# A hybrid S5 / FNet / attention step on one core: TensorE's queue in the order of the source, the other queues as the scheduler sets them

## The chip, the core and the metric

The kernel runs on one core of one Trainium2 chip. The metric is the device time of one execution in microseconds (us), as the median of several runs.

## What is computed

The reference is one inference step of a model of two layers, for 128 context tokens and 1024 latent tokens of width 1024, in float32. Cut to what matters here, a layer is:

```python
def mixer_layer(x, cvec, lw, ctx_kv, ssm_h0, rope):
    shift, scale, gate = adaln(cvec, ada_w, ada_b)
    h = rmsnorm(x, norm_g) * (1.0 + scale) + shift
    a_in, a_gate, f_in, f_gate, q, k, v, c_gate = jnp.split(h @ w_in, SPLITS, axis=-1)
    ya, finals = s5_mixer(a_in, a_re, a_im, log_dt, b_re, b_im, c_re, c_im, d_skip, h0_f, h0_b)
    za = jax.nn.gelu(ya) @ glu_w
    ya = za[..., :BRANCH_W] * jax.nn.sigmoid(za[..., BRANCH_W:])
    yf = fourier_mix(f_in) @ fnet_w
    q = rmsnorm(q.reshape(b, s, N_HEADS, HEAD_DIM), q_gain)
    k = rmsnorm(k.reshape(b, s, N_KV, HEAD_DIM), k_gain)
    yc = blocked_attention(apply_rope(q, cos, sin), k_all, v_all)
    branches = jnp.stack([ya * silu(a_gate), yf * silu(f_gate), yc * silu(c_gate)], axis=2)
    proj = jnp.einsum('bsnw,nwd->bsnd', branches, w_branch)
    g = jax.nn.sigmoid(h @ merge_w + merge_b)
    return x + gate * (jnp.sum(g * proj, axis=2) @ w_out), k, v, finals
```

So there are large dense products (`w_in`, `glu_w`, `fnet_w`, `merge_w`, `w_branch`, `w_out`) and three branches of many small steps: a state-space branch, a Fourier branch and attention with 8 heads. `adaln` is a product of one vector with a matrix of 1024 x 3072.

## The kernel before

**Tiles.** The 1152 tokens stand in the free dimension in three tiles of 384, the channels on the 128 partitions. Each float32 operand is kept as a rounded part and a remainder (`hh` and `hl`, `whi` and `wlo`), and a product is three matmuls of 128x384 (`mm3`, L162). A block of dense output is made in units by the generator `dense` (L269): weights are loaded (`wst`), split by ScalarE (`whi`) and GpSimd (`wlo`), and after each 12 matmuls into a `pd` buffer it yields. An evacuation on ScalarE or VectorE (`jo`) and a DMA follow each `pd`.

**PSUM.** There are four names of buffers: `pd` (2, dense), `pt` (2), `pv` (1) and `pa` (1, three banks). The three branches and the setup share `pt`, `pv` and `pa`.

**What is traced.** The branches are generators too, and `drive` (L92) traces two or three of them in turn by the costs that they yield. The stages of a layer (`layer`, L1289) are: dense blocks beside the state-space setup, state inputs and scans; `qkv_gen` (L837) beside dense blocks; `ssm_out_gen` (L738) beside dense blocks; `glu`; `fnet_gen` (L1001) beside three dense blocks; `attn_gen` (L1089) with the merge blocks, 12 matmuls between two steps; the output blocks beside the norm of the next layer (`h_gen`, L470). `run` (L1541) traces the head ahead of that: the constants, the loads of x, one step of `ada_gen` (L306), the transposes of x (`x_gen`, L398), the rest of `ada_gen` with the first normalized tiles.

**What sets the order.** The tracing order is not the order of the queues. The scheduler of the tile framework takes the traced instructions and sets the order of each engine's queue by its own model of when they get ready and when buffers come free. On TensorE that moves dense matmuls between the steps of a branch and branch steps between dense matmuls.

The lines that the change touches are `mm` (L167), which issues every matmul, and `tr` (L170), which issues every transpose; the helpers `act` (L134), `tt` (L144) and `stt` (L147) for ScalarE, VectorE and GpSimd, and `dma` (L124), stay as they are. Steps named further on:

- `qkv_gen`: `tail()` (L912) transposes the rotated heads of one token tile (`qk_kk`, `qk_qt`) into `pa`, copies them out (`qk_qo`) on ScalarE and stores them. The tail of tile t-3 is traced after the projection of tile t. The last ones follow each other in the trace.
- `fnet_gen`: for each of four channel groups, load `fn_X`, even and odd sums `fn_EO` (six operations on VectorE), an alternating sum `fn_s`, folded sums `fn_G` (eight operations), the channel transform into `pt`, its split `fn_AB`, the position transform into `pa`, and the sums of the result (`fn_s`, `fn_X` again) with the split into `A`.
- `ssm_out_gen`: coefficients `ss_CK` on VectorE, `toeplitz` (L763) with small matmuls into `pt`, a way through DRAM (`tpd`) back as `ss_TT`, a copy `ss_TP`, the output products into `pa` and `pv`.
- `attn_gen`: `scores` (L1112) into `pa`, a softmax (`at_mx`, `at_P`), `trans` (L1123) with nine transposes, and for each second step `pvm` (L1135).
- `h_gen`: the sum of squares (`ssq`) by `ones` into `pv`, the scales `rs`, their transposes.

Of the kernel before, what the change touches and what calls it, by code (L numbers as in the profile page):

```python
# [101 lines left out]
class Program:  # L102
# [62 lines left out]
        self.mm(out, w[1], x[0], False, last)  # L165

    def mm(self, out, w, x, first=True, last=True, **kw):  # L167
        return self.nc.tensor.matmul(out, w, x, start=first, stop=last, **kw)  # L168

    def tr(self, out, in_, ident=None):  # L170
        i = self.ident if ident is None else ident
        n = in_.shape[0]
        return self.nc.tensor.transpose(out, in_, i[:n, :n])  # L173


    def setup(self):
# [1418 lines left out]
```

## Time and profile before

| | us |
|---|---|
| median of 3 runs (2752.75 to 2756.11) | 2754.29 |
| the profiled execution | 2752.03 |
| its span, first to last instruction | 2750.3 |
| TensorE matmuls and transposes busy | 2627.0 (96%) |
| TensorE weight loads busy (beside the matmuls) | 2509.0 (91%) |
| VectorE | 1826.6 (66%) |
| ScalarE | 1143.5 (42%) |
| GpSimd | 683.4 (25%) |

The mean granted TensorE clock is 0.985 of full speed. PE stands for TensorE, DVE for VectorE, ACT for ScalarE, POOL for GpSimd, SP for the engine that issues most DMAs. A wait is the idle time of an engine just before an instruction; the name behind the arrow is what ended last before it. A row of the timeline gives start and length in us; neighbours of one kind are drawn together with their count, and the ends of matmuls overlap the next start, so starts tell the pace.

### The profile page before, as it was taken

How to read it: one execution, taken by the hardware profiler on the slowest of the kernel's cores; microseconds unless marked ns; L12 is line 12 of the kernel's file. 1: busy time of each engine (PE TensorE's matmuls, PEld its weight loads, DVE VectorE, ACT ScalarE, POOL GpSimd, SP SyncE). 2: the span in 40 equal slices, each digit the busy share in tenths (PEclk: the TensorE clock that was granted, in tenths of full speed). 3: DMA queues.
4: the chain of work that ended last, by engine and by line, in shares of the span. 5: the costliest groups of instructions: out<-in, count | busy, mean ns of one | idle time of the engine just before them, and what ended most of it. 6: DMA issues, size and time to landing. Idle time of an engine off the chain costs nothing. (4 is left out here: it accounts for less than half of the span.)

```text
span 2750.3 us, 44553 instructions
## 1 busy us (share of the span) xinstructions
PE 2627.0 (96%) x16092; PEld 2509.0 (91%) x16092; DVE 1826.6 (66%) x3933; ACT 1143.5 (42%) x2676; POOL 683.4 (25%) x521
## 2 busy tenths in 40 slices
PE   7998999899999999999999899999999999999998
PEld 3898999799999999999989899989989998999998
DVE  6549955856558889866572797577654788891343
ACT  5461145331355565423345322543223655553244
POOL 3241122322321020132343212233222202102223
PEclk9999999999999999999999999999999999999999
DMA  6632223566263345544543222345645334433244
GB/s 223 178 99 84 95 87 110 150 191 207 86 202 114 110 138 153 173 126 114 165 146 93 95 89 84 107 125 160 211 154 174 109 121 150 143 121 98 80 121 149
DMA packets 459997, 366.85 MB, mean 133 GB/s; under 512 B 72953, under 2 KB 432001, under 8 KB 459777
## 3 DMA queue, kind: packets, MB, share of 16 engines
q1 hardware_dynamic: 458480, 359.75, 42.9%
q0 software_dynamic: 1296, 4.26, 0.5%
q8 instruction: 127, 2.08, 0.3%
q14 instruction: 94, 0.76, 0.1%
HBM read 243.52 MB, written 120.39 MB: 132 GB/s over the span
## 5 line engine op out<-in xcount | busy, mean ns | idle before, releaser
L168 PE MATMUL pd<-hh,whi 128*128 128x384 f32 x2496 | 857.1, 344 | 24.0 <-ACT jo L142 20.1
L168 PE MATMUL pd<-hh,wlo 128*128 128x384 f32 x2496 | 844.6, 339 | 3.2 <-POOL wlo L145 3.2
L168 PE MATMUL pd<-hl,whi 128*128 128x384 f32 x2496 | 843.1, 338 | 1.3 <-DVE hl L149 1.3
L145 POOL TENSOR_TENSOR wlo<-wst,whi 128x512 fp32r<-128x512 f32 x312 | 437.9, 1405 | 1525.8 <-ACT whi L142 1404.8
L168 PEld LDWEIGHTS pd<-hh,whi 128*128 128x128 f32 x2496 | 472.5, 189 | 35.0 <-ACT jo L142 22.8
L168 PEld LDWEIGHTS pd<-hh,wlo 128*128 128x128 f32 x2496 | 472.5, 189 | 7.8 <-POOL wlo L145 5.7
L168 PEld LDWEIGHTS pd<-hl,whi 128*128 128x128 f32 x2496 | 473.1, 190 | 3.8 <-DVE hl L149 2.3
L168 PE MATMUL pd<-A,whi 128*128 128x384 f32 x1728 | 458.2, 342 | 8.2 <-ACT jo L142 4.9
L168 PEld LDWEIGHTS pd<-A,whi 128*128 128x128 f32 x1728 | 311.2, 189 | 11.7 <-ACT jo L142 5.6
L142 ACT ACTIVATE whi<-wst 128x512 fp32r<-128x512 f32 x312 | 196.0, 630 | 278.5 <-PE pd L168 190.6
L168 PE MATMUL pd<-A,wlo 128*128 128x384 f32 x864 | 293.9, 340 | 0.0
L1078 DVE TENSOR_REDUCE at_mx<-pa 128x1 f32<-128x1152 f32 x128 | 173.3, 1354 | 16.1 <-PE pa L168 15.7
L168 PE MATMUL pa<-at_K,at_Q 128*128 128x384 f32 x768 | 167.2, 347 | 8.6 <-ACT at_P L142 5.8
L142 ACT ACTIVATE at_PT<-pt 128x384 fp32r<-128x384 f32 (+1 forms) x260 | 114.9, 490 | 144.0 <-PE pt L173 143.6
L142 ACT ACTIVATE at_P<-pa,at_mx 128x1152 f32<-128x1152 f32 x128 | 158.1, 1235 | 20.7 <-DVE at_mx L1078 19.4
L168 PEld LDWEIGHTS pd<-A,wlo 128*128 128x128 f32 x864 | 163.2, 189 | 0.1
L168 PEld LDWEIGHTS pa<-at_K,at_Q 128*128 128x128 f32 x768 | 128.3, 188 | 29.0 <-ACT at_P L142 25.5
L168 PE MATMUL pt<-qkW,hh 128*128 128x384 f32 x576 | 150.7, 343 | 0.0
L168 PE MATMUL pv<-at_PT,at_V 128*128 128x256 f32 x1152 | 148.8, 283 | 0.0
L168 PEld LDWEIGHTS pv<-at_PT,at_V 128*128 128x128 f32 x1152 | 144.7, 191 | 0.8
L142 ACT ACTIVATE jo<-pd 128x384 f32<-128x384 f32 x120 | 58.0, 485 | 198.1 <-PE pd L168 96.5
L145 DVE TENSOR_TENSOR at_PT<-pt,at_PT 128x384 fp32r<-128x384 f32 (+1 forms) x260 | 133.1, 550 | 10.0 <-ACT at_PT L142 7.8
(294 smaller groups left out, 3772.3 us busy)
## 6 DMA issues: line engine op xcount, KB each, us to landing
aw<-in_ada_w_dram SPq DMA_DIRECT2D x48, 512.0 KB, 4.8
wst<-in_merge_w_dram SPq DMA_DIRECT2D x96, 256.0 KB, 3.0
wst<-in_w_in_dram SPq DMA_DIRECT2D x80, 256.0 KB, 2.9
td<-jo SPq DMA_DIRECT2D x96, 192.0 KB, 2.3
jt<-td SPq DMA_DIRECT2D x96, 192.0 KB, 2.8
wst<-in_w_out_dram SPq DMA_DIRECT2D x64, 256.0 KB, 2.9
sgd<-jo SPq DMA_DIRECT2D x72, 192.0 KB, 2.0
jt<-sgd SPq DMA_DIRECT2D x64, 192.0 KB, 2.7
```

The costliest lines, as they stand in the source:

```text
L142: return self.nc.scalar.activation(out, in_, func, **kw)
L145: return (e or self.nc.vector).tensor_tensor(out=out, in0=a, in1=b, op=op)
L168: return self.nc.tensor.matmul(out, w, x, start=first, stop=last, **kw)
L1078: nc.vector.tensor_reduce(out=mx[:, 0:1], in_=src, axis=AX.XY if m3 else AX.X, op=OP.max, negate=True)
```

## The change

Every matmul and every transpose that the program traces is handed to `keep_in_program_order`: TensorE's queue then has these instructions in the order in which the source traces them. Nothing else is pinned; VectorE, ScalarE, GpSimd and the DMA queue get their orders from the scheduler as before. No instruction is added and none is taken away.

```diff
     def mm(self, out, w, x, first=True, last=True, **kw):
-        return self.nc.tensor.matmul(out, w, x, start=first, stop=last, **kw)
+        return self.tc.keep_in_program_order(self.nc.tensor.matmul(out, w, x, start=first, stop=last, **kw))
 
     def tr(self, out, in_, ident=None):
         i = self.ident if ident is None else ident
         n = in_.shape[0]
-        return self.nc.tensor.transpose(out, in_, i[:n, :n])
+        return self.tc.keep_in_program_order(self.nc.tensor.transpose(out, in_, i[:n, :n]))
```

What this does to TensorE's queue is shown at three places, first before and then with the change. In these rows `pt`, `pv`, `pa` and `pd` are the PSUM buffers that are written.

The head, from the queue's second row on: `ident,hl_77` to `hl_79` are the transposes of x (24 for each tile of 384 tokens), `fvst` that of the small vectors, `aw,silc` and `awr,sc` the matmuls of `ada_gen` with its weights. Before:

```order
L173 MATMUL pt<-ident,hl_77 128x128 x8
L173 MATMUL pv<-ident,fvst 128x128
L173 MATMUL pt<-ident,hl_77 128x128 x16
L173 MATMUL pt<-ident,hl_78 128x128 x24
L173 MATMUL pt<-ident,hl_79 128x128 x24
L168 MATMUL pa<-aw,silc 4x512
L168 MATMUL pa<-awr,sc_108 4x512 x2
```

With the change:

```order
L173 MATMUL pv<-ident,fvst 128x128
L168 MATMUL pa<-aw,silc 4x512
L173 MATMUL pt<-ident,hl_77 128x128 x24
L173 MATMUL pt<-ident,hl_78 128x128 x24
L173 MATMUL pt<-ident,hl_79 128x128 x24
L168 MATMUL pa<-awr,sc_108 4x512 x2
L168 MATMUL pa<-aw,silc 4x512
```

The first matmul of `ada_gen` has moved from behind the 72 transposes of x to ahead of them.

The last tails of the first half of `qkv_gen` in layer 0, with the numbers of the buffers: `pa_4580` to `pa_4670` are the tails of the last four tiles, `pv_4694` that of the cached keys, `pd_4726` is a dense block. Before:

```order
L173 MATMUL pa_4580<-identr_81,qk_kk_4441 128x128 x4
L173 MATMUL pa_4580<-identr_81,qk_qt_4438 128x128 x2
L168 MATMUL pd_4726<-hh0_345,whi_4037 128x384
L168 MATMUL pd_4726<-hl0_346,whi_4037 128x384
L168 MATMUL pd_4726<-hh0_345,wlo_4038 128x384
L168 MATMUL pd_4726<-hh0_345,whi_4037 128x384
L168 MATMUL pd_4726<-hl0_346,whi_4037 128x384
L168 MATMUL pd_4726<-hh0_345,wlo_4038 128x384
L168 MATMUL pd_4726<-hh0_345,whi_4037 128x384
```

With the change:

```order
L173 MATMUL pa_4580<-identr_81,qk_kk_4441 128x128 x4
L173 MATMUL pa_4580<-identr_81,qk_qt_4438 128x128 x2
L173 MATMUL pa_4623<-identr_81,qk_kk_4528 128x128 x4
L173 MATMUL pa_4623<-identr_81,qk_qt_4525 128x128 x2
L173 MATMUL pa_4657<-identr_81,qk_kk_4611 128x128 x4
L173 MATMUL pa_4657<-identr_81,qk_qt_4608 128x128 x2
L173 MATMUL pa_4670<-identr_81,qk_kk_4654 128x128 x4
L173 MATMUL pa_4670<-identr_81,qk_qt_4651 128x128 x2
L173 MATMUL pv_4694<-identr_81,qk_kk_4691 128x128 x4
```

The dense block and the projection of the second half's first tile, which stood between the tails, have moved behind the last of them.

The Fourier stage of layer 0, at the end of a group: `dftp,fn_ABp` is the last matmul of the group's position transform, `dftc,fn_G` the first of the next group's channel transform, `pd` a dense block. Before:

```order
L168 MATMUL pa<-fn_t_7175,fn_AB 128x2x128
L168 MATMUL pa<-dftp,fn_ABp 128x128 x2
L168 MATMUL pd<-hh_347,whi 128x384
L168 MATMUL pd<-hl_348,whi 128x384
L168 MATMUL pd<-hh_347,wlo 128x384
L168 MATMUL pd<-hh_347,whi 128x384
```

With the change:

```order
L168 MATMUL pa<-fn_t_7175,fn_AB 128x2x128
L168 MATMUL pa<-dftp,fn_ABp 128x128 x2
L168 MATMUL pt<-dftc,fn_G 128x128 x4
L168 MATMUL pd<-hh_347,whi 128x384
L168 MATMUL pd<-hl_348,whi 128x384
L168 MATMUL pd<-hh_347,wlo 128x384
```

Before, some 40 dense matmuls stand between the two groups; with the change the next group's first four transform matmuls follow at once, and in the two later groups 12 dense matmuls stand between.

## Rows read from the trace of the kernel before

**Rows 1.** The page: span, and busy time of each engine

```profile
span 2750.3 us, 44553 instructions
...
PE 2627.0 (96%) x16092; PEld 2509.0 (91%) x16092; DVE 1826.6 (66%) x3933; ACT 1143.5 (42%) x2676; POOL 683.4 (25%) x521
```

**Rows 2.** Waits of PE, whole kernel: line <- awaited: us in total, times, longest

```profile
PE pd L168 <- ACT jo L142: 25.1, 8, 7.8
...
PE pt L173 <- DVE at_P L1082: 8.4, 13, 1.0
...
PE pt L168 <- DVE fn_G L145: 6.3, 9, 0.9
```

**Rows 3.** Windows: us, PE PEld DVE ACT POOL busy, PEclk, DMA share, GB/s

```profile
49.60:63.30 13.70, 9.83 (x20) 2.40 (x21) 8.18 (x15) 7.24 (x14) 10.46 (x7) 0.50 0.42 116
220.30:230.50 10.20, 5.57 (x17) 5.57 (x18) 9.61 (x34) 1.60 (x4) 1.27 (x1) 0.50 0.20 64
418.30:421.70 3.40, 3.40 (x15) 3.40 (x14) 3.05 (x8) 1.37 (x4) 1.19 (x1) 0.50 0.52 155
414.00:428.50 14.50, 11.99 (x72) 11.21 (x71) 8.13 (x22) 8.10 (x27) 4.52 (x4) 0.88 0.65 188
432.00:442.00 10.00, 10.00 (x60) 10.00 (x59) 3.50 (x8) 5.03 (x27) 1.33 (x1) 1.00 0.18 56
2030.00:2100.00 70.00, 67.08 (x430) 64.58 (x429) 36.95 (x94) 23.60 (x50) 22.96 (x14) 1.00 0.33 106
```

**Rows 4.** Timeline, PE, Fourier stage: start us, length us, instruction [idle before]

```profile
696.68 0.60 PE L168 MATMUL pa<-dftp,fn_ABp 128*128 128x128 f32 x4
...
713.98 0.61 PE L168 MATMUL pa<-dftp,fn_ABp 128*128 128x128 f32 x4
...
727.81 0.60 PE L168 MATMUL pa<-dftp,fn_ABp 128*128 128x128 f32 x4
```

**Rows 5.** Timeline, DVE, the same stage: the fn_G of three groups

```profile
703.55 5.08 DVE L145 TENSOR_TENSOR fn_G<-fn_EO 128x192 f32<-128x192 f32 x8
...
720.87 2.92 DVE L145 TENSOR_TENSOR fn_G<-fn_EO 128x192 f32<-128x192 f32 x8
...
735.80 3.97 DVE L145 TENSOR_TENSOR fn_G<-fn_EO 128x192 f32<-128x192 f32 x8
```

**Rows 6.** Timeline, PE, tails of q/k/v in layer 0

```profile
414.17 0.46 PE L173 MATMUL pa<-identr,qk_kk 128*128 128x128 f32 x4
...
414.64 0.41 PE L168 MATMUL pd<-hh,whi 128*128 128x384 f32 x1
...
428.08 0.34 PE L173 MATMUL pv<-identr,qk_kk 128*128 128x128 f32 x2
```

**Rows 7.** Timeline, PE, head

```profile
8.48 1.94 PE L173 MATMUL pt<-ident,hl 128*128 128x128 f32 x8 [8.48 <-DMA dmask<-in_k_dmask_dram]
...
24.50 1.02 PE L168 MATMUL pa<-aw,silc 128*4 128x512 f32 x2
...
52.80 0.59 PE L168 MATMUL pa<-awr,sc 128*4 128x512 f32 x1 [3.60 <-POOL awr L145]
```

**Rows 8.** Timeline, PE, state-space output of layer 0

```profile
487.65 1.03 PE L168 MATMUL pt<-ss_CK,ss_B 128*32 128x240 f32 x8 [3.36 <-issue]
...
505.91 0.51 PE L168 MATMUL pa<-ssU,ss_TP 128*128 128x145 f32 x2 [0.98 <-ACT ss_TP L142]
...
532.40 0.76 PE L168 MATMUL pa<-ss_Hg,ss_CA 128*128 128x145 f32 x4 [2.32 <-DVE ss_Hg L805]
```

**Rows 9.** Lines, 766 to 1145 us: instruction, shapes, count | busy us, mean ns | idle

```profile
L1078 DVE TENSOR_REDUCE at_mx<-pa 128x1 f32<-128x1152 f32 x64 | 86.6, 1354 | 8.0 <-PE pa L168 7.8
...
L142 ACT ACTIVATE at_P<-pa,at_mx 128x1152 f32<-128x1152 f32 x64 | 79.0, 1235 | 10.4 <-DVE at_mx L1078 9.7
```

**Rows 10.** Timeline, PE, two long waits

```profile
224.93 0.69 PE L168 MATMUL pd<-hh,whi 128*128 128x384 f32 x1 [7.84 <-ACT jo L142]
...
1412.53 1.41 PE L168 MATMUL pv<-ones,ssq 128*128 128x1 f32 x6 [4.20 <-DVE ssq L145]
```

## The prediction

> **What bounds the kernel now.** I read the page's head and block of busy times first. TensorE matmuls are busy 2627.0 us of a span of 2750.3 us [rows 1]: TensorE is the bound nearly everywhere, and all its idle time together is 123 us. A better order could win at most that, and most of it stands in a few places; an order that leaves TensorE standing where it now works costs one for one. Next come the waits of TensorE [rows 2]. They are short: the largest sum is 25.1 us in 8 waits for a copy of ScalarE, then waits of about 0.7 us each in attention and in the Fourier stage. So the chains that run over VectorE, ScalarE and a DMA are hidden now, because the scheduler put dense matmuls (`pd`) between the steps of a chain. The question is what each chain hides behind when the steps of TensorE stand as they are traced. The orders of the changed kernel answer where: on VectorE, ScalarE, GpSimd and the DMA queue the chains stand nearly as before, and on TensorE the order is the same in most dense stretches, but not in the head, at the tails of q/k/v, at the start of the state-space output, in the Fourier stage, in attention and at the end of a layer. Last I read the granted clock [rows 3]: at full clock 60 matmuls and transposes take 10.0 us (0.167 us each, 2.0 us for a dense piece of 12), and after waits there are stretches at 0.50 (1.2 GHz), where they take about twice as long.
>
> **What the change does, place by place.** It adds and removes no arithmetic; the work displaced from one place is done in another. What it costs is the TensorE time that is not covered any more, at full clock.
>
> *Fourier stage, twice.* For three of the four channel groups the chain is: last `pa` matmul, then VectorE's `fn_s`, `fn_X`, `fn_EO`, `fn_s`, then eight `fn_G` subtractions, each feeding two transform matmuls into `pt`. The `pa` rows end at 697.28, 714.59 and 728.41 (start plus length) [rows 4]. The first of the eight `fn_G` is done at 703.55 + 5.08/8 = 704.2, at 720.87 + 0.37 = 721.2 and at 735.80 + 0.50 = 736.3 [rows 5]: chains of 6.9, 6.6 and 7.9 us, together 21.4. Before, dense pieces filled them. In the pinned order 0, 12 and 12 dense matmuls stand there, 4.0 us by the row of rows 3; 17.4 us stay open. Eight `fn_G` take 5.08, 2.92 and 3.97 us against some 2 us of matmuls that wait for them; beyond the first op and the piece of 12 that now stands inside the first group that is another 2.3. Against 19.7 stand the waits that are there already, 6.3 us in both layers [rows 2], 3.2 a layer. **+16.5 a layer**, ends 12 (the chain shorter, since no dense evacuations are on VectorE meanwhile) and 23 (nothing of the 4.0 helps).
>
> *Tails of q/k/v, twice.* Transposes of rotated heads into the one `pa` buffer stand at 414.17 and three places more, and `pv` ends it at 428.08 [rows 6]. Between two of them lie ScalarE's copy `qk_qo` and the stores. In these 14.5 us TensorE was busy 11.99 [rows 3], 2.0 of it the transposes themselves (six within 0.47 us, to the dense row at 414.64 [rows 6], four times, and the `pv`). The other 10.0 us were dense and q-projection matmuls, 3.4 us of that at clock 0.50 [rows 3], so worth 8.3 at full clock. All of it now stands behind the last transpose. **+9 a layer**, ends 6 (the copies come faster when ScalarE has no dense evacuations) and 12.
>
> *Head, once.* The first ada matmul is traced before the transposes of x and now stands ahead of all 72. It needs the first weight tile, which is loaded behind x; it ran without a wait at 24.50, after transposes that began at 8.48 [rows 7], so the tile was there somewhat earlier. If the transposes begin at 22 to 24 in place of 8.48, and take most of the 16.0 us that they took there, they end at 36 or later. Part comes back: ada waited 3.60 at 52.80 [rows 7] and ran 13.7 us at half clock [rows 3], which with weights waiting in place may go. **+8**, ends 2 (half clock gone too) and 16 (the whole 24.50 - 8.48).
>
> *State-space output, twice.* Products of `ss_CK` into `pt` stand between dense pieces from 487.65 to 505.91, with waits of 3.36 and 0.98 in the rows [rows 8]; four second halves of dense pieces (8 us) now stand behind. The later wait of 2.32 at 532.40 [rows 8] takes some back: **+5 a layer**, ends 2 and 8.
>
> *Attention, twice.* Between the scores of one step and the transposes of the step before lie a maximum of 1.354 us and an exponential of 1.235 us [rows 9] and the scaling; two or three dense matmuls fewer cover it on every other step. It waits now 13 times for the scaled probabilities, 8.4 us in all [rows 2], so the cover is nearly exact. **+3 a layer**, ends 0 and 10.
>
> *End of a layer.* The 4.20 us wait for `ssq` at 1412.53 [rows 10] stays; the transposes of the scale rows move up behind it. **+3**, ends 1 and 7.
>
> *Clock.* A wait that is now bare can be followed by a stretch of 3.4 us at 0.50 as at 418.3 [rows 3], which loses 1.7. The tails, the head and the state-space output have theirs already. The Fourier stage has none in layer 1, where the clock was 1.00 for 70 us [rows 3], so I take four new ones: **+7**, ends 0 and 34 (below).
>
> The clock rule of the Trainium skill speaks against the change: its page "TensorE: Matmul & The Clock Gate", section "HAM oscillation — how this bites in real kernels", says that waits between bursts of matmuls throw the array back to half rate burst after burst. The trace agrees only in part: in those 70 us TensorE stood still for 2.92 [rows 3], and the clock stayed at 1.00; by the rule the sum is the fourth rival's, by the row it is mine.
>
> **The sum.** 2 x 16.5 + 2 x 9 + 8 + 2 x 5 + 2 x 3 + 3 + 7 = +85. The profiled execution took 2752.03 us (span 2750.3, 1.7 around it), 2.3 below the median of 2754.29; put on the median it is **2839 us**. All low ends together give +43, all high ends but the clock's +136; 8 in 10 of this case lie in 2808 to 2870.
>
> **The rivals.** *First, faster.* The two longest waits of TensorE, 7.84 us at 224.93 [rows 10] and its like in layer 1, end with ScalarE's copy `jo`, which stands behind other copies in ScalarE's queue. The scheduler of ScalarE sees another TensorE order and might put `jo` first. That gives back 15.7 us, and the two stretches of 10.2 us at half clock there [rows 3] another 10: with no new bare wait 2754 - 26 = 2728 us. It decides only while the new waits stay under 26 us, and in the changed order ScalarE has these copies where they were. *Second, the chains are shorter than they look,* because their lengths in the trace hold dense evacuations on the same engines: all terms at their low ends but the Fourier stage at 10, +39, 2793 us. For: `fn_X` and `fn_G` vary by nearly two (5.08 against 2.92 us [rows 5]). Against: their shortest sum is still over 5 us. *Third, attention opens.* If each of the 64 pairs of steps loses 0.8 us in place of 13 losing 0.65, this is +51 in place of +6: 2884 us. Against: every second step keeps a value product in between, and the dense piece of each step stays between its transposes and the next scores. *Fourth, the clock falls after each bare wait:* some 20 new ones (6 Fourier, 8 tails, 4 state-space, head, end of layer) times 1.7 is +34 in place of +7: 2866 us. *Fifth, the pin does nothing,* 2754 us: against it, TensorE's order differs, and a queue that waited 7.84 us in one place does not go round a waiting matmul.
>
> **How the numbers follow.** Forecast 0.55, second 0.18, fourth 0.12, third 0.08, first 0.04, fifth 0.03. The range 2785 to 2890 takes in the forecast's bounds, the second and the fourth, and part of the third; outside are the first, the fifth, a slice of the second and of the third. A difference under 0.2% (5.5 us) can't be told from none. Faster by more: the first and a trace of the second, 0.05; within: the fifth and a little, 0.04; slower: the rest, 0.91.
>
> **What would show it.** Right: TensorE's busy time about as before and its idle time about 200 us; waits for `fn_G` or `fn_s` of 5 to 8 us, six times, the largest of all; waits for `qk_qo` above 15 us in sum; the first transposes of x behind the first ada matmul; some 35 to 50 us of the loss before the end of layer 0's Fourier stage. Wrong: waits for `fn_G` under 2 us each (the dense pieces still cover), waits for `at_P` above 30 us (third), or the 7.84 us gone (first).

## The result and the profile after

The changed kernel takes 2903.56 us (median of 4 runs, 2900.02 to 2908.60) against 2753.64 us of the kernel before in the same comparison: a ratio of 1.0544, 95% interval 1.0526 to 1.0563, some 150 us slower. The direction was as forecast; the forecast of 2839 us and the upper end of the range, 2890, were too low.

The page of the profiled execution after, with the head and the busy times that answer to [rows 1]:

```profile
span 2906.8 us, 44552 instructions
...
PE 2648.2 (91%) x16092; PEld 2542.3 (87%) x16092; DVE 1808.2 (62%) x3933; ACT 1147.6 (39%) x2676; POOL 673.6 (23%) x521
```

TensorE's busy time has risen by 21 us (2648.2 against 2627.0) and its idle time within the span by 135 us (258.6 against 123.3). VectorE, ScalarE and GpSimd do the same work in a longer span. The mean granted clock fell from 0.985 to 0.965.

TensorE's waits after, by what they ended with (total us, times, longest), which answer to [rows 2]:

```profile
PE pt L168 <- DVE fn_G L145: 42.2, 9, 7.1
PE pd L168 <- ACT jo L142: 25.5, 8, 7.8
PE pa L173 <- ACT qk_qo L142: 24.5, 8, 5.8
PE pa L168 <- DMA aw<-in_ada_w_dram: 12.9, 1, 12.9
PE pv L173 <- DMA ss_ld<-in_ssm_a_re_dram: 12.8, 1, 12.8
...
PE pv L168 <- DVE at_PT L145: 9.2, 17, 0.8
...
PE pa L168 <- ACT ss_TP L142: 7.9, 2, 4.0
PE pa L168 <- DVE ss_Hg L805: 7.8, 6, 2.4
PE pa L173 <- ACT A L142: 7.7, 4, 1.9
PE pt L173 <- ACT A L142: 7.7, 4, 1.9
PE pv L168 <- DVE ssq L145: 6.6, 1, 6.6
...
PE pt L173 <- DVE at_P L1082: 5.4, 7, 1.5
```

The wait for `jo` is the same as before (25.5 against 25.1). That for `fn_G` went from 6.3 to 42.2. Most of the others in this list were shorter or absent before (`qk_qo` 5.8 in sum, `ss_TP` 1.6, `ssq` 4.2, `ss_Hg` 6.4); that for `at_P` fell, from 8.4 to 5.4.

Where the time came in is read from the starts of TensorE's instructions: at the borders of the stages both queues have the same matmul at the same place, so the time between two such starts can be compared. The profiled execution after is the slowest of its four (2908.60 us), so these differences add up to 156.5 us, where the medians are 150 apart. "Idle" is the sum of TensorE's waits in a stretch; "rest" is what remains of the difference, which is matmuls that ran slower.

| stretch of the kernel before, us | what runs there | before | after | more | of it idle | rest | forecast |
|---|---|---|---|---|---|---|---|
| 0 to 140 | head, first dense blocks | 140.1 | 163.0 | 22.9 | 24.1 | -1.2 | 8 |
| 405 to 470 | tails of q/k/v, layer 0 | 65.0 | 74.5 | 9.6 | 8.2 | 1.3 | 9 |
| 480 to 600 | state-space output, layer 0 | 120.1 | 127.8 | 7.8 | 5.7 | 2.1 | 5 |
| 690 to 765 | Fourier stage, layer 0 | 75.1 | 94.9 | 19.7 | 17.8 | 2.0 | 16.5 |
| 765 to 1150 | attention, layer 0 | 384.9 | 391.8 | 6.9 | 6.8 | 0.0 | 3 |
| 1400 to 1540 | end of layer 0 | 139.9 | 146.2 | 6.2 | 6.6 | -0.5 | 3 |
| 1750 to 1780 | tails of q/k/v, layer 1 | 30.0 | 39.4 | 9.4 | 8.9 | 0.6 | 9 |
| 1822 to 1910 | state-space output, layer 1 | 87.7 | 96.5 | 8.9 | 6.5 | 2.3 | 5 |
| 2025 to 2110 | Fourier stage, layer 1 | 84.9 | 108.1 | 23.2 | 16.6 | 6.6 | 16.5 |
| 2110 to 2495 | attention, layer 1 | 385.0 | 394.7 | 9.6 | 8.5 | 1.2 | 3 |
| 2695 to the end | last output blocks, final norm | 55.1 | 75.7 | 20.6 | 14.2 | 6.3 | 0 |

The other stretches together make 12 us, 5 of them from 1150 to 1400 us. The clock, which the forecast counted by itself with 7, is in the column of the rest.

**Fourier stage.** TensorE's timeline at three of the group ends (start, length, instruction, idle before), which answers to [rows 4]:

```profile
739.10 0.60 PE L168 MATMUL pa<-dftp,fn_ABp 128*128 128x128 f32 x4
746.41 0.77 PE L168 MATMUL pt<-dftc,fn_G 128*128 128x128 f32 x2 [6.71 <-DVE fn_G L145]
...
759.07 0.60 PE L168 MATMUL pa<-dftp,fn_ABp 128*128 128x128 f32 x4
...
768.69 3.76 PE L168 MATMUL pt<-dftc,fn_G 128*128 128x128 f32 x16 [6.93 <-DVE fn_G L145]
...
780.11 0.60 PE L168 MATMUL pa<-dftp,fn_ABp 128*128 128x128 f32 x4
...
789.36 3.75 PE L168 MATMUL pt<-dftc,fn_G 128*128 128x128 f32 x16 [6.56 <-DVE fn_G L145]
```

From the end of the last `pa` matmul to the first `fn_G` matmul it takes 6.7, 9.0 and 8.6 us (739.70 to 746.41, 759.67 to 768.69, 780.71 to 789.36), against chains of 6.9, 6.6 and 7.9 that were read from the trace before. TensorE's waits just ahead of these `fn_G` matmuls are 6.71, 6.93 and 6.56; in the second and third gap the 12 dense matmuls fill the rest.

**Head.** TensorE's timeline, and then the DMA queue's, from the first ada matmul to the first transpose of `ss_ld`, with the queue's longest wait from 50 to 95 us as the last line; it answers to [rows 7]:

```profile
23.06 1.87 PE L168 MATMUL pa<-aw,silc 128*4 128x512 f32 x2 [12.86 <-DMA aw<-in_ada_w_dram]
...
38.16 0.66 PE L173 MATMUL pt<-ident,hl 128*128 128x128 f32 x4 [0.35 <-DVE A L415]
...
91.72 0.28 PE L173 MATMUL pv<-ident,ss_ld 32*128 32x32 f32 x1 [12.84 <-DMA ss_ld<-in_ssm_a_re_dram]
```

```profile
63.26 5.83 SPq L127 DMA_DIRECT2D xTd<-A  x6
89.78 0.33 SPq L127 DMA_DIRECT2D ss_ld<-in_ssm_a_re_dram  x1
...
SPq L127 <- DVE hl L149: 20.1, 1, 20.1
```

The first ada matmul ran at 23.06, after a wait of 12.86 for its weights, and the transposes ended near 38.8 in place of 24.5. Then comes a second wait, 12.84 at 91.72, for the load of `ss_ld`. The DMA queue issued that load at 89.78, 20 us after the last of the stores ahead of it. Before the change it was issued at 82.35 and the transposes ran at 85.14, without a wait, with dense matmuls ahead of them. What held the queue in those 20.1 us was VectorE: the wait ends with the last `hl` of the head's normalized tiles, written from 88.07 to 89.22. I read it as a buffer in memory that the head uses until then (the load goes out late in both kernels); the buffer was not tried by itself.

**Last output blocks.** TensorE's timeline of three blocks after and then of two before:

```profile
2860.73 0.55 PE L173 MATMUL pa<-ident,A 128*128 128x128 f32 x3 [1.91 <-ACT A L142]
...
2868.93 0.55 PE L173 MATMUL pa<-ident,A 128*128 128x128 f32 x3 [1.91 <-ACT A L142]
...
2875.57 0.44 PE L173 MATMUL pt<-ident,A 128*128 128x128 f32 x2 [1.91 <-ACT A L142]
```

```profile
2718.12 0.54 PE L173 MATMUL pa<-ident,A 128*128 128x128 f32 x3
...
2722.68 0.54 PE L173 MATMUL pa<-ident,A 128*128 128x128 f32 x3
```

Each transposes the result of the dense block just finished, as it was traced. Ahead of it TensorE waits 1.91 us, for an evacuation on VectorE, then a square and a scaling on ScalarE. A block then takes 6.64 us (2868.93 to 2875.57), and 8.20 where the clock was low (2860.73 to 2868.93); in the kernel before, with the transposes one piece of 12 matmuls later, 4.56. These two blocks of the pinned kernel as windows (as in [rows 3]; the granted clock is the third number from the end):

```profile
2860.73:2868.93 8.20, 6.29 (x28) 5.97 (x28) 1.67 (x3) 2.40 (x4) 2.55 (x2) 0.79 0.31 93
2868.93:2875.57 6.64, 4.73 (x28) 4.41 (x28) 1.67 (x3) 2.40 (x4) 2.55 (x2) 1.00 0.34 102
```

### The profile page after: what moved, and what is told of

The parts are those of the page before. It is cut to its first block, busy times and chain, and to the rows that moved or that the text cites. A ratio compares the mean times of both kernels' runs of the same rounds, so it can differ in the third digit from the quotient of the medians.

```text
span 2906.8 us, 44552 instructions
## 1 busy us (share of the span) xinstructions
PE 2648.2 (91%) x16092; PEld 2542.3 (87%) x16092; DVE 1808.2 (62%) x3933; ACT 1147.6 (39%) x2676; POOL 673.6 (23%) x521
## 5 line engine op out<-in xcount | busy, mean ns | idle before, releaser
L168 PE MATMUL pd<-hh,whi 128*128 128x384 f32 x2496 | 867.2, 347 | 21.8 <-ACT jo L142 20.2
L168 PEld LDWEIGHTS pd<-hh,whi 128*128 128x128 f32 x2496 | 478.9, 192 | 32.4 <-ACT jo L142 23.2
L142 ACT ACTIVATE at_P<-pa,at_mx 128x1152 f32<-128x1152 f32 x128 | 158.4, 1237 | 12.9 <-DVE at_mx L1078 12.7
L168 PEld LDWEIGHTS pv<-at_PT,at_V 128*128 128x128 f32 x1152 | 141.8, 191 | 19.5 <-ACT at_P L142 15.5
```

The source lines that it names most:

```text
L142: return self.nc.scalar.activation(out, in_, func, **kw)
L168: return self.tc.keep_in_program_order(self.nc.tensor.matmul(out, w, x, start=first, stop=last, **kw))
```

## The experiments

Each kernel below is compared with the kernel before in its own runs; "us against the pinned kernel" is the difference of the two ratios (to 1.0544) times 2754. The 95% interval of most ratios is some 5 us wide to either side, so a difference from the pinned kernel under about 7 us can't be told from none.

**1. The head.** In the pinned kernel:

```diff
-            next(ada)
             self.run_all(self.x_gen(xT, ssq))
+            next(ada)
```

> The pinned kernel, with the first ada step traced behind the transposes of x in place of ahead of them; all else pinned. Theory (the pinned order costs what is bare behind an instruction that waits, place by place): the 12.9 us wait for the first weight tile and the late transposes go, the ada matmuls end about 10 us sooner; the later wait of 12.8 us for ss_ld stays. 2903.6 - 10 = 2893 us. Rival (the head is bounded by its weight loads whatever the order): within 3 us of 2903.6, with the same time of the first dense matmul.

Measured 2899.47 us, ratio 1.0513 (1.0480 to 1.0546): about 9 us less, which its wide interval doesn't set clear of noise. The trace does: just behind the head TensorE's instructions start 9.3 us sooner (6.1 of it is left at the end), and the wait for `ss_ld` is 13.36 us. So the head has two costs of about that size, and this takes away one.

**2. The last output blocks.** The transposes of block b (`tails(b)` traces the three) stand where block b+1 is evacuated:

```diff
+                            if b:
+                                tails(b - 1)
+                            if b == 7:
+                                tails(7)
...
-                            for i in range(3):
-                                self.tr(self.tail[i][b // 4][:, 128 * (b % 4):128 * (b % 4) + 128], xo[:, b, 768 + 128 * i:896 + 128 * i])
```

> The pinned kernel, with the transposes of the last output blocks traced one dense block later, so that 24 dense matmuls stand between an evacuation and the transposes that read it. Theory: the waits of 1.9 us before these transposes (seven in the last stage) and the half clock behind them go; TensorE's lag on the kernel before grows by 20 us in this stage, so 2903.6 - 18 = 2886 us. Rival (the lag comes from the clock or from the queues of the other engines): under 5 us.

Measured 2888.34 us, ratio 1.0483 (1.0464 to 1.0502): 17 us less. The blocks stand 4.5 us apart again:

```profile
2853.51 0.49 PE L173 MATMUL pa<-ident,A 128*128 128x128 f32 x3
...
2858.01 0.49 PE L173 MATMUL pa<-ident,A 128*128 128x128 f32 x3
```

**3. The Fourier stage left to the scheduler,** all else pinned:

```diff
+            self.pin = False
             drive((self.dense(3), 48), (self.fnet_gen(l, f_d, zt["f"]), 48))
+            self.pin = True
```

> The pinned kernel, with the instructions of the Fourier stage (three dense blocks and the Fourier branch, both layers) not pinned, so that the scheduler sets them. Theory: the 42 us waits for fn_G fall to the 6 of the kernel before, both layers give back 19 and 23 us: 2903.6 - 40 = 2864 us. Rival (what is won there is lost later, at the head of attention): 2885 or more.

Measured 2865.40 us, ratio 1.0398 (1.0377 to 1.0418): 40 us less. The row of its waits for `fn_G` (`pin` adds lines, so numbers shift) is that of the kernel before:

```profile
PE pt L169 <- DVE fn_G L146: 6.3, 9, 0.9
```

**4. Bare waits filled.** Behind a group's last `pa` matmul, for three groups of each layer:

```diff
+            if g < 3:
+                fill = self.pst("pv")
+                for i in range(24):
+                    self.mm(fill[:, :384], self.dftl[0][:, 0, :128], self.hh[0][:, 0])
```

> The pinned kernel with 24 more matmuls, whose result nobody reads, in each of the three bare waits of the Fourier stage of each layer. They take 4.1 us of a wait of 6.6 to 7 us at full clock. Theory with a share of the clock: the waits stay covered, the stretches at half clock behind them (24 us in layer 0, 20 in layer 1) go, and with them 8 to 20 us: about 2890 us. Rival (the clock has no share, the chain on VectorE alone paces the stage): 2901 to 2906. Third (the waits were no free room): 24 more, 2928.

Measured 2910.10 us, ratio 1.0563 (1.0540 to 1.0587): 5 us more, within the noise, and in none of the three expected ranges; the nearest is the rival's. The windows (us, five engines' busy times, granted clock, DMA) of the same stretch of the pinned kernel, and then of this one:

```profile
745.00:755.00 10.00, 8.10 (x40) 7.79 (x41) 5.40 (x13) 2.22 (x5) 2.53 (x2) 0.64 0.05 20
...
765.00:775.00 10.00, 6.31 (x32) 6.32 (x33) 6.49 (x20) 1.20 (x2) 1.71 (x2) 0.66 0.08 25
```

```profile
745.00:755.00 10.00, 6.83 (x36) 6.62 (x37) 5.90 (x16) 1.96 (x5) 3.50 (x2) 0.83 0.03 10
...
765.00:775.00 10.00, 6.47 (x29) 6.18 (x29) 7.63 (x19) 2.29 (x4) 3.53 (x3) 0.70 0.14 46
```

The clock is higher, 0.83 in place of 0.64, but the stage isn't shorter: the group ends stand 19.5, 22.7 and 20.5 us apart (740.07, 759.53, 782.22, 802.67) against 20.0, 21.0 and 20.6. So 144 matmuls more, about 25 us at 0.173 us each, cost about 5: the waits are room (those for `fn_G` fall from 42.2 to 19.4 us). It suggests that the low clock behind them costs little here, because the stage goes by VectorE's chain. But the filler also moves the dense pieces and their evacuations deeper into that chain, so this doesn't measure the clock's share. How much of the whole loss is due to the clock is not settled: the "rest" of the table, some 21 us in all, is what slower matmuls added to TensorE's busy time.

**5. The tails of q/k/v** between the projections of the second half (`cl`, `ch` and `cp` are the tails, projections and code carried over from the first half):

```diff
+                if half and t < 3:
+                    cl.pop(t + 6)()
+                    if t == 0:
+                        cl[8] = cp(8, *ch.pop(8))
+                    yield 400
```

> The pinned kernel, with the last three tails of q/k/v's first half and that of the cached keys traced between the projections of the second half, so that each has a projection of 24 matmuls between it and the next. Theory (bare waits, place by place): the 24 us waits for qk_qo go, both layers give back 9.5 us, 2903.6 - 17 = 2887 us. Rival (the copies and stores of the tails bound the stage): under 5 us.

Measured 2905.63 us, ratio 1.0545 (1.0529 to 1.0561): nothing. TensorE's waits in the tails of layer 0, pinned kernel and then this one:

```profile
PE pa L173 <- ACT qk_qo L142: 10.7, 3, 5.8
```

```profile
PE pv L173 <- ACT qk_kk L142: 5.4, 1, 5.4
PE pt L168 <- POOL qkW L145: 1.5, 2, 0.9
PE pt L168 <- ACT qkW L142: 1.4, 1, 1.4
```

The waits for `qk_qo` went. In their place stand the cached keys (5.4: their split and transposes are traced together) and the weights of the second half (`qkW`). I read the second as a matter of buffers: `qkW` has one set, its split starts when the first half's last projection ends, and the bare tails had covered it. That was not tried by itself; experiment 9, which changes both, loses under 1 us in these stretches.

**6. The state-space output** left to the scheduler:

```diff
+                    self.pin = False
                     drive((self.dense(6), 12*6), (self.ssm_out_gen(l, a_d, y_d), 33), (self.qtail_gen(), QT))
+                    self.pin = True
```

> The pinned kernel, with the state-space output stage (six dense blocks, the branch and the last q tails, both layers) left to the scheduler. Theory: the 8.6 and 9 us lost there come back, 2903.6 - 15 = 2888 us. Rival (the loss there is a loss by the clock or is taken back at the next stage): 2898 or more.

Measured 2891.35 us (2886.89 to 2899.06), ratio 1.0503 (1.0477 to 1.0529): 11 us less. In its profiled execution, one of its two fastest, some 8 us come back at the stage in layer 0 and 9 at that in layer 1; the spread of its runs is larger than that of most others, and the median shows less.

**7. The Fourier stage pinned alone,** the rest left to the scheduler:

```diff
-        self.pin = True
+        self.pin = False
...
+            self.pin = True
             drive((self.dense(3), 48), (self.fnet_gen(l, f_d, zt["f"]), 48))
+            self.pin = False
```

> The kernel before, with the instructions of the Fourier stage alone pinned. Theory (each place costs for itself): as much more than the kernel before as the pinned kernel loses there, 19 + 23 us: about 2796 us. Rival (the loss needs the pinned neighbours): under 2770.

Measured 2799.01 us, ratio 1.0157 (1.0140 to 1.0174): 43 us more than the kernel before. Its trace lies 2 us behind that of before at 679 us, 21 at 750, 26 at 2033 and 49 at 2098. The place costs for itself what it costs in the pinned kernel.

**8. Attention and merges** left to the scheduler:

```diff
+            self.pin = False
             for k in self.attn_gen(l, qs_d, k_d, v_d, sg_d[2], zc_d):
                 self.run_some(m, k)
             run(m)
+            self.pin = True
```

> The pinned kernel, with attention and the merge blocks beside it left to the scheduler, both layers. Theory: the 7 and 10 us lost there come back, 2903.6 - 16 = 2888 us. Rival (attention drifts by some us with the phase in which it starts, whatever the order): 2897 or more.

Measured 2895.62 us, ratio 1.0511 (1.0493 to 1.0530): 9 us less, just clear of noise, between theory and rival. The first layer gives back 6 to 7 us, the second 2 to 4. In the pinned kernel the value product waits 9 times, 5.0 us, for the last split `at_PT` in layer 0 alone; here once, for 1.4, but the wait for `at_P` rises from 2.7 to 6.7. So which wait makes attention's loss is not shown.

**9. The source traced anew at six places,** still pinned: experiments 1, 2 and 5 (the cached keys two projections later, a higher cost yielded while the second half's weights are split), and three other costs:

```diff
+        if l == 0:
+            yield 830
-            yield 2000 if x == 0 else 1200
+            yield 4500 if x == 0 else 3000 if x == 1 else 700
-            yield 500
+            yield 6000 if g else 500
```

(`ssm_setup_gen`, `ssm_out_gen`, `fnet_gen`; a yielded cost decides how many dense pieces `drive` traces next. Two further such costs, in `fnet_gen` and in the share of `ssm_setup_gen` in `drive`, are changed too and not printed.)

> The pinned kernel with its source traced anew at six places, so that dense matmuls stand in the bare waits: the first ada step behind the transposes of x, the transposes of ss_ld six dense pieces later, the tails of q/k/v between the projections of the second half (and that of the cached keys two projections later), three pieces between two Fourier groups, more pieces ahead of the first products of the state-space output, the transposes of the last output blocks one block later. Theory (a pinned order is as good as the order in which the source is traced): of the 150 us some 110 come back, what stays is attention, 17, and the ends of layers: 2785 to 2805 us. Rival (the pinned order costs by itself, since nothing answers to waits any more): above 2840.

Measured 2807.89 us, ratio 1.0191 (1.0174 to 1.0208): 97 us less, just above the theory's range. TensorE's waits:

```profile
PE pd L168 <- ACT jo L142: 25.6, 8, 7.8
PE pa L168 <- ACT ss_TP L142: 15.1, 4, 4.1
PE pt L168 <- DVE fn_G L145: 11.0, 7, 2.8
...
PE pv L168 <- DVE at_PT L145: 9.5, 18, 0.5
...
PE pa L173 <- ACT qk_qo L142: 5.0, 4, 1.5
```

`fn_G` is down to 11.0, `qk_qo` to 5.0, `ss_ld` and `aw` are out of the list. `ss_TP` rose from 7.9 to 15.1: as I read it, more dense pieces ahead of the first products put those late, and with them what goes through DRAM. The state-space stages were not mended: in this trace they lose about 6 and 11 us. TensorE's busy time is 2625.3 us, as before the change.

**10. The same source without pins:**

```diff
-        return self.tc.keep_in_program_order(self.nc.tensor.matmul(out, w, x, start=first, stop=last, **kw))
+        return self.nc.tensor.matmul(out, w, x, start=first, stop=last, **kw)
```

and the same in `tr`.

> The kernel before (nothing pinned) with the same source traced anew. Theory (the scheduler orders TensorE by its own model and the tracing order only breaks ties): within 8 us of the kernel before, 2746 to 2762 us. Rival (the tracing order carries into the scheduled one): another time than the kernel before by more than 10 us.

Measured 2760.61 us, ratio 1.0024 (1.0015 to 1.0034), 7 us more than the kernel before and within the theory's range: in its trace about 5 us are lost in each state-space stage (it waits 12.9 us for `ss_TP`), 4 and 2 won in the Fourier stages. So on this source the pin still costs 47 us (2807.89 against 2760.61); by the traces some 8 of them come between 765 and 1400 us (attention of layer 0 and what follows), 6 at the end of layer 0 and 12 between 2110 and 2695 us, places that the retracing left as they were.

**11. The first rival's price:** `ss_fin` on VectorE, nothing pinned. In the kernel before, ScalarE stood 12.25 us ahead of this copy until VectorE's scan was done, with the `jo` copies behind it:

```profile
223.66 0.32 ACT L142 ACTIVATE ss_fin<-A 128x64 f32<-128x64 f32 x1 [12.25 <-DVE A L145]
```

The edit:

```diff
-        self.act(fin, H[:, :, :, 16])
+        self.nc.vector.tensor_copy(fin, H[:, :, :, 16])
```

> The kernel before (nothing pinned), with the copy ss_fin of the scan's final states on VectorE in place of ScalarE, where it stood ahead of the copies of dense results. This prices the first rival of the prediction. Theory: the two waits of 7.84 and 7.83 us for jo go and the stretches at half clock with them: 15.7 to 26 us less than the kernel before, 2728 to 2739 us. Rival (the dense results run ahead and TensorE waits later for the scan): within 6 us of the kernel before.

Measured 2736.03 us, ratio 0.9929 (0.9916 to 0.9943): 20 us less; in its trace 10.6 in each layer, 3.7 of it lost again by the end. The wait for `jo` is:

```profile
PE pd L168 <- ACT jo L142: 8.6, 6, 2.2
```

**12. A version that beats both:** 11 with the source of the q/k/v tails and of the Fourier stage from 9 (with the diff of 5), nothing pinned:

```diff
-            yield 500
+            yield 6000 if g else 500
...
-        self.act(fin, H[:, :, :, 16])
+        self.nc.vector.tensor_copy(fin, H[:, :, :, 16])
```

> The kernel before (nothing pinned), with ss_fin on VectorE, the last tails of q/k/v traced between the projections of the second half, and three dense pieces traced between two Fourier groups. Theory (the tracing order of those two stages carried into the scheduled one in the kernel with everything traced anew, where its lag fell by 1.5 and 3.9 us in layer 0 and 3.3 and 1.6 in layer 1): 8 to 10 us less than the kernel with ss_fin alone. Rival (that was drift): the same time as with ss_fin alone, within 4 us.

Measured 2725.28 us, ratio 0.9889 (0.9875 to 0.9902): 31 us less than the kernel before and 11 less than experiment 11.

## Why the prediction was wrong

**Right: the mechanism and most places.** A pinned queue stands still where the next instruction in the source waits, and the loss is what was hidden there. Experiments 3 and 7 show it both ways for the Fourier stage (-40, +43), 6 for the state-space output, 9 for the whole: retracing gives back 97 of 150 us with the pins in place, so for these it is the tracing order that costs and not the pin. The tails (9.6 and 9.4 against 9) and the Fourier stage (19.7 and 23.2 against 16.5 and a share of the clock) were well sized. Most signs came true: waits for `fn_G` the largest sum, `qk_qo` at 24.5 us, the transposes of x behind the first ada matmul. But TensorE's idle time is 259 us in place of about 200, and 62 us were lost before the end of layer 0's Fourier stage in place of 35 to 50.

**Wrong step: the head, priced at one place of two.** "+8, ends 2 and 16" took the 72 transposes and hoped for a refund from ada's own waits. Experiment 1 shows that term at 9. What the sum left out is the second place of the head: the transposes of `ss_ld` stand behind the first 12 dense matmuls in the pinned order, and their load goes out only at 89.78, when VectorE has written the head's last tile. It is a bare wait of 12.84 us, and the retracing of 9 takes it away (TensorE lies 5.5 us behind the kernel before at 189 us, against 25.5).

**Wrong step: no term for the last output blocks.** The prediction has none: it passed over transposes that moved up by one piece of 12 matmuls. Experiment 2 shows 17 us, for eight waits of 1.9 us in a row, each paid in full because 2 us of cover was all there was. With this one place mended the kernel takes 2888.34 us, just inside the forecast's range.

**Mis-sized: attention, the state-space output, the end of layer 0.** Attention lost 6.9 and 9.6 against 3 a layer, within the end of 10. The wait for the scaled probabilities, on which the term was built, did not grow (8.4 before, 5.4 after); the largest new one is that for the split `at_PT` ahead of the value product (9.2 after). The state-space output lost 7.8 and 8.9 against 5: nothing came back at the later wait (2.4 us in place of 2.32), and that for `ss_TP` grew from 0.98 to 4.0. The end of layer 0 lost 6.2 against 3, with 6.6 us for `ssq` in place of 4.20.

**The clock term** of 7 was too small if all of the 21 us more of busy time is the clock's; of the fourth rival's 34 the rows bear out at most two thirds. The Trainium skill's page "TensorE: Matmul & The Clock Gate", section "HAM oscillation — how this bites in real kernels", says that when the wait ahead of each burst of matmuls is long enough, each burst starts at half rate anew. The trace agrees where the waits are long: behind the wait of 6.93 us the `fn_G` matmuls from 768.69 on ran at a granted clock of 0.50. Where they are short it goes both ways: behind the same wait of 1.91 us one output block ran at 0.79 and the next at 1.00. So the 2.92 us of short waits in 70 us, which the prediction held against that rule, were no test of it. Experiment 4, where the clock rose and the time did not fall, suggests that a stage paced by VectorE's chain pays little for a low clock.

**The first rival** was right in its price (26 at most; 20 measured in experiment 11, which brings it by another edit) and wrong that this change could bring it: ScalarE kept its order, and the two waits of 7.8 us stayed.

## What to carry to other kernels

A queue pinned to the source is as good as the order in which the source is traced: before pinning, list each place where the next instruction waits for a chain and give it as much other work, in the source, as the chain takes; small moves count, where the cover was exact. Price a pinned order from the order listing place by place and to the end of the program, loads whose buffers come free late included. And look at what stands at the head of the other queues: one copy that waited on ScalarE (`ss_fin`) was worth 20 us, which neither order of TensorE's queue touched.

## What the runs showed of the hardware

TensorE's granted clock fell to half also where no wait was long: in the last output blocks, with a wait of 1.9 us in each, two of the five blocks from 2860.73 to 2897.08 (the first and the last) hold stretches at half clock and three do not. Before the change a stretch at 0.50 began at 418.30 [rows 3], just behind a wait of 1.93 us for `qk_qo`. In the pinned kernel the clock was at half for about 200 us in all (0.035 of full speed missing over 2907 us, twice), against 83 before. Filling bare waits with matmuls raised the clock (0.64 to 0.83 from 745 to 755 us) and won nothing (2910.10 us against 2903.56).
